# A decoder block in fp32 on one core: another order in the mixer, an earlier split of a weight block, a root with a bias at the end

## The chip, the cores and the metric

The kernel runs on one core of a Trainium2 chip. The metric is the time of one execution on the device in microseconds (us), the median of several runs. Its engines work beside each other, each through its own list of instructions in order: TensorE (PE) multiplies matrices, VectorE (DVE), ScalarE (ACT) and GpSimd (POOL) do the elementwise work, and SyncE (SP) issues the transfers between the main memory and the on-chip buffer SBUF. PE writes its results into eight banks of PSUM. PEld is the part of PE that loads the stationary operand of the next matmul while the present one runs.

## The reference

One token block of 256 rows and 1024 columns goes through a decoder block in fp32:

```
u = rmsnorm(h, norm_mix_pre)
z = u @ w_in                          # p (512) | q (512) | k (512) | v (512) | g (2048)
g = z[..., o_g:] + b_gate;  g_pool, g_attn = g[..., :1024], g[..., 1024:]
y_pool = pool_mixer(p, pool_w, pool_scale) @ w_branch_pool      # causal means over 2, 4, 8, 16 rows
y_attn = moba_attention(q, k, v) @ w_branch_attn                # 256 rows are one block: causal, ALiBi, 8 heads
m = sigmoid(g_pool) * y_pool + sigmoid(g_attn) * y_attn
h = h + rmsnorm(m @ w_out, norm_mix_post)
u2 = rmsnorm(h, norm_mlp_pre)
a = square(relu(u2 @ w_up))                                     # 4096 columns
h = h + rmsnorm(a @ w_down, norm_mlp_post)                      # the output
```

## The kernel before

Every product is made of three matmuls, since each fp32 operand is kept as a rounded part `hi` and a remainder `lo`: hi by hi, lo by hi, hi by lo (`mm3`, L227 to L229; `mm3_wide` with 512 columns, L236 to L240). Weights come from the main memory in blocks of 1 MB, issued by SP into three raw buffers. Each block is split when its turn comes: ACT writes `hi` (L89), and then `lo = raw - hi` (L93) is written by DVE alone, or for most blocks ahead of the MLP by DVE (11/16 of the columns, 1408 per partition) and POOL (5/16, 640 per partition) side by side (`share_lo`). `split_next` takes the next block in the order of use, and issues the load of another into the raw buffer that comes free.

The order on every engine is the order of the code; nothing reorders it. A tile waits for its producers by semaphores.

The stages, in the order in which PE meets them:

- v, q and k. `features(blocks, f2, ...)` makes 256 output columns (a group of 48 matmuls of 256 moving columns, with the weights stationary and the tokens `u` moving). Its hook `early` runs before the splits that it calls, `evac` after them. `evac_k` (L483) multiplies the keys with the row factor on DVE (L434), writes them as `hi` on ACT (L489) and as `lo` on DVE (L490) into the tile `stacked`.
- scores (L522, L523) of two heads at a time, softmax on DVE and ACT, with the slopes of ALiBi in the tile `prob`, filled by POOL (`fill_slopes`, L441).
- p, two groups; between them and behind them fp32 transposes of the probabilities (`turn_probs`).
- the gates, g0 to g3, each of two blocks and two groups of 48 matmuls, written below as g00, g01, g10 and so on to g31. Between them lie the fp32 matmuls of the attention (`attend`), the transposes of probabilities and of the attention's output (`turn_attended`, L316), and `pool_project`, the four small products y of the pooling groups.
- the branch products: `bp` from the pooled y (`yh`, `yl`) and `ba` from the attention (`oT`), four groups of 24 matmuls each, then the output projection, and the MLP with its 8 chunks of 512 columns up and down. In the down product each token tile has two PSUM banks of 512 columns; the last piece of a chunk runs as twelve matmuls of 256 columns (`mm3_quarters`).
- `finish(t)` for each of two token tiles: the squares are summed on ACT, DVE multiplies the gain in, the root follows, and three passes (L876) of 384, 384 and 256 columns scale the rows and add the residual; each is sent out by SP (L877). The second half of the gain is divided between DVE (256 columns) and ACT with POOL (256 columns, L872, L873).

`placed(pool, blocks, tag, name, at)` allots a tile and begins its data `at` elements in, so that its address can be chosen against that of other operands.

Of the kernel before, what the change touches and what calls it, by code (L numbers as in the profile page):

```python
# [16 lines left out]
P = 128  # L17
D = 1024
# [15 lines left out]
def hybrid_block(ctx: ExitStack, tc: tile.TileContext, x, norm_mix_pre, w_in, b_gate, pool_w, pool_scale,  # L34
# [229 lines left out]
    def placed(pool, blocks, tag, name, at, room=128):  # L264


        t = pool.tile([P, blocks * S + room], F32R, tag=tag, name=name)
        return t[:, at:at + blocks * S].rearrange("p (k s) -> p k s", k=blocks)
# [4 lines left out]
    def halves():  # L273
        return [(n, slice(n * 512, (n + 1) * 512)) for n in range(2)]
# [151 lines left out]
    def turn_factors():  # L426
        rps = bank("rr_ps")
        for t in range(NT):
            nc.tensor.transpose(rps[:, t * P:(t + 1) * P], spread[:, t * P:(t + 1) * P], ident)
        nc.vector.tensor_copy(rrow, rps[:, 0:S])  # L430
# [8 lines left out]
    def fill_slopes(heads, eng):  # L439
        for h in heads:  # L440
            eng.tensor_scalar(prob[:, h, :], dist, 2.0 ** (-8.0 * (h + 1) / H), None, op0=ALU.mult)  # L441
# [6 lines left out]
    def features(blocks, f2, evac, name, ahead=2, early=None):  # L448
        ps = bank(f"{name}_ps{f2}")
        for j in range(2):  # L450
            for k in range(KD):
                feature(ps, j, blocks, 2 * f2 + j, k)
        if early:
            early(2 * f2, ps)
        if f2 == 0:
            split_next(ahead)
        if evac:
            evac(2 * f2, ps)
        return ps
# [41 lines left out]
    for f2 in range(2):  # L501
        for k in range(KD):
            feature(qps[f2], 1, bq, 2 * f2 + 1, k)
        evac_q(2 * f2, qps[f2])
    turn_factors()
    fill_slopes(range(4, H), nc.gpsimd)
    features(bk, 0, None, "k", early=evac_k)
    k_ps1 = features(bk, 1, None, "k")


# [37 lines left out]
    def attend(po, hp):  # L548
        for h in range(2 * hp, 2 * hp + 2):
            c = slice(h * DH, (h + 1) * DH)  # L550
            nc.tensor.matmul(po[0][:, c], pTs[h][:, 0:P], v_sb[:, 0, c], start=True, stop=True, skip_group_check=True)
            nc.tensor.matmul(po[1][:, c], pTs[h][:, P:2 * P], v_sb[:, 0, c], start=True, stop=False,
                             skip_group_check=True)
            nc.tensor.matmul(po[1][:, c], pTs[h][:, 2 * P:3 * P], v_sb[:, 1, c], start=False, stop=True,
                             skip_group_check=True)
# [11 lines left out]
    def turn_attended():  # L567
        for t in range(NT):
            c = slice(t * P, (t + 1) * P)
            ps = turn(o_sb[:, t, :], 0, f"ot_ps{t}")  # L570
            parts(oT[0][:, :, c], oT[1][:, :, c], ps.rearrange("p (f s) -> p f s", f=4))
# [40 lines left out]

    def pool_project(g2):
        if not yp:
            yp.extend(placed(mixer, NG, t, t[2:], a) for t, a in (("q_yh", 0), ("k_yl", 16)))
        ps = bank(f"y_ps{g2}")
        for j in range(2):
            g = 2 * g2 + j
            mm3(ps[:, j * S:(j + 1) * S], (pws[0][:, g, :], pws[1][:, g, :]), (ys[0][:, g, :], ys[1][:, g, :]),
                True, True)  # L620
        for j in range(2):
            g = 2 * g2 + j
            v, sc = ps[:, j * S:(j + 1) * S], others[P_SCALE + g]
            nc.scalar.activation(yp[0][:, g, :], v, AF.Copy, scale=sc)
            nc.vector.scalar_tensor_tensor(yp[1][:, g, :], v, sc, yp[0][:, g, :].bitcast(F32),
                                           op0=ALU.mult, op1=ALU.subtract)
# [14 lines left out]
    def gates(i, f2):  # L641
        def evac(f, ps):
            c = 4 * i + f
            for j in range(2):
                nc.scalar.activation(sg[:, c + j, :], sg[:, c + j, :], AF.Sigmoid, bias=others[B_GATE + c + j])

        def early(f, ps):
            by_token(sg[:, 4 * i + f:4 * i + f + 2, :], ps)
            if (i, f2) == (3, 1):
                begin_split()()  # L650
        features(bg[i], f2, evac, f"g{i}", early=early)
# [15 lines left out]
    pool(0)  # L667
    pool(1)
    gates(0, 0)
    attend(po, 0)  # L670
    attend(po, 1)
    gates(0, 1)
    pool(2)
    pool(3)
    turn_probs(2)
    turn_probs(3)
    gates(1, 0)
    attend(po, 2)
    attend(po, 3)
    attended(po)  # L680
    ys_pws = mixer.tile([P, 2, NG, S + P], F32R, tag="prob", name="ys_pws")
    ys = [ys_pws[:, i, :, 0:S] for i in range(2)]
    pws = [ys_pws[:, i, :, S:S + P] for i in range(2)]
    gates(1, 1)
    turn_attended()
    split_pool()
    gates(2, 0)
    pool_project(0)
    gates(2, 1)
    pool_project(1)  # L690

    def broadcast(src, name):
        t = const.tile([P, D], F32, name=name)
# [160 lines left out]
    def finish(t):  # L854

        o = o_out[:, t, :]
        ss = small.tile([P, 3], F32, name="ss")
        rr = small.tile([P, 1], F32, name="rr")

        def gain(a, b):  # L860
            nc.vector.scalar_tensor_tensor(o[:, a:b], pd[t][a // 512][:, a % 512:a % 512 + b - a], r2[t],
                                           g_mlp_post[:, a:b], op0=ALU.mult, op1=ALU.mult)

        nc.gpsimd.memset(ss[:, 2:3], 0.0)
        sumsq_act(pd[t][0], ss[:, 0:1], r2[t])
        gain(0, 512)
        sumsq_act(pd[t][1], ss[:, 1:2], r2[t])
        chain = rstd(ss, rr)
        next(chain)
        next(chain)  # L870
        gain(512, 768)
        nc.scalar.activation(o[:, 768:D], pd[t][1][:, 256:512], AF.Copy, scale=r2[t])  # L872
        nc.gpsimd.tensor_tensor(o[:, 768:D], o[:, 768:D], g_mlp_post[:, 768:D], ALU.mult)  # L873
        run(chain)
        for a, b in ((0, 384), (384, 768), (768, D)):
            nc.vector.scalar_tensor_tensor(o[:, a:b], o[:, a:b], rr, h_sb[:, t, a:b], op0=ALU.mult, op1=ALU.add)  # L876
            nc.sync.dma_start(out[0, t * P:(t + 1) * P, a:b], o[:, a:b])  # L877

    prev, nxt = a0, a1
    for j in range(NCH):  # L880
        last = j == NCH - 1
        for t, k in [(t, k) for t in range(NT) for k in range(4)]:
            if last and t == NT - 1:
                continue
            if not last and (t, k) == (NT - 1, 3):

                mm3_quarters(pd[t], tokens(prev, k, t), wide(bd[j], k))
            else:
                mm3_wide(pd[t], tokens(prev, k, t), wide(bd[j], k), j == 0 and k == 0, last and k == 3)
        split_next(2)  # L890
        if last:
            break
        if j + 2 < NCH:
            a = up_parts(j + 2)
            up_half(j + 2, 0, a)
            up_half(j + 2, 1, a)
        else:
            a = None
        prev, nxt = nxt, a
    finish(0)  # L900
    for n, c in halves():
        for k in range(4):
            h, l = wide(bd[-1], k)
            mm3(pd[1][n], tokens(prev, k, 1), (h[:, c], l[:, c]), False, k == 3)
    finish(1)


# [27 lines left out]
```

## Time and profile before

| | |
|---|---|
| runs, us | 343.43, 343.54, 344.56; median 343.54 |
| the profiled execution | 343.66, of which the span of the trace is 341.89 |
| granted TensorE clock, mean over the span | 0.996 |
| PE busy | 332.6 us, 97% of the span, 2355 matmuls |
| DVE, ACT, POOL busy | 220.7 (65%), 182.8 (53%), 77.3 (23%) |
| moved by DMA | 63.04 MB, mean 184 GB/s |

Times in the rows are in us from the start of the span. A matmul's duration overlaps the next one's, so the rate of PE is read from one start to the next, or from the length of a stretch that holds a whole group. A stretch's count of matmuls takes in those that reach into it, two or three more than were started there.

### The profile page before, as it was taken

What the parts mean: (1) busy time and instruction counts of PE and PEld (TensorE: products, weight loads), DVE (VectorE), ACT (ScalarE), POOL (GpSimd) and SP (SyncE); (2) the same over time, 40 slices, a digit from 0 to 9 for tenths busy, and PEclk for the clock granted to TensorE, in tenths of its full rate; (3) what the DMA queues carried; (4) which work ended last, traced back from release to release, by engine and by line L of the source; (5) the groups of instructions that cost most, each with busy time, mean ns of one, the idle gap of its engine ahead of it and who ended that gap; (6) DMA issues with size and microseconds to landing.
All of it is one profiled execution on the core that took longest, in us unless ns stands there. A gap on an engine that the chain in (4) does not pass through costs nothing.

```text
span 341.9 us, 5763 instructions
## 1 busy us (share of the span) xinstructions
PE 332.6 (97%) x2355; PEld 308.6 (90%) x2355; DVE 220.7 (65%) x288; ACT 182.8 (53%) x257; POOL 77.3 (23%) x70
## 2 busy tenths in 40 slices
PE   8999999999999999999999999999999999999990
PEld 6799999999999999888898998989989899899880
DVE  3799697996476699466686746637366373653545
ACT  3985658765655755076668426354263551644231
POOL 3699965154303000046700000000000000000000
PEclk9999999999999999999999999999999999999998
DMA  7996961654545946806355763907629177180003
GB/s 215 372 314 221 205 227 35 233 153 158 183 166 204 326 168 217 276 1 246 125 156 214 277 215 133 331 29 261 231 83 339 71 247 246 40 330 3 0 0 123
DMA packets 27506, 63.04 MB, mean 184 GB/s; under 512 B 1332, under 2 KB 3160, under 8 KB 27480
## 3 DMA queue, kind: packets, MB, share of 16 engines
q1 hardware_dynamic: 26904, 62.15, 53.0%
q0 software_dynamic: 576, 0.52, 1.2%
q8 instruction: 18, 0.29, 0.3%
q14 instruction: 8, 0.07, 0.1%
HBM read 61.10 MB, written 1.05 MB: 182 GB/s over the span
## 4 chain that ended last, share of the span: by engine, by line
PE 84%; DVE 5%; DMA 4%; ACT 2%; SPq 1%; POOL 1%; issue 1%; DVEq 0%; ACTq 0%; POOLq 0%
PE up_ps L227 9%; PE up_ps L228 9%; PE up_ps L229 9%; PE d_ps L237 7%; PE d_ps L236 7%; PE d_ps L240 7%; PE g_ps L227 4%; PE g_ps L228 4%; PE g_ps L229 4%; DMA v_r<-in_w_in_dram 2%; PE wo_ps L240 2%; PE wo_ps L236 2%; PE wo_ps L237 2%; DMA k_r<-in_w_in_dram 2%; DVE k_l L93 1%; PE bp_ps L228 1%
## 5 line engine op out<-in xcount | busy, mean ns | idle before, releaser
L227 PE MATMUL up_ps<-u2h,up_h 128*128 128x256 f32 x224 | 62.1, 277 | 0.0
L228 PE MATMUL up_ps<-u2l,up_h 128*128 128x256 f32 x224 | 61.9, 276 | 0.0
L229 PE MATMUL up_ps<-u2h,up_l 128*128 128x256 f32 x224 | 61.9, 276 | 0.0
L93 DVE TENSOR_TENSOR dn_l<-dn_r,dn_h 128x2048 fp32r<-128x2048 f32 x16 | 36.5, 2292 | 16.7 <-ACT dn_h L89 16.6
L228 PEld LDWEIGHTS up_ps<-u2l,up_h 128*128 128x128 f32 x224 | 42.1, 188 | 0.0
L227 PEld LDWEIGHTS up_ps<-u2h,up_h 128*128 128x128 f32 x224 | 42.1, 188 | 0.0
L229 PEld LDWEIGHTS up_ps<-u2h,up_l 128*128 128x128 f32 x224 | 42.1, 188 | 0.0
L89 ACT ACTIVATE dn_h<-dn_r 128x2048 fp32r<-128x2048 f32 x16 | 30.5, 1918 | 21.5 <-issue 12.8
L236 PE MATMUL d_ps<-dn_h,ah 128*128 128x512 f32 x106 | 41.3, 390 | 0.0
L237 PE MATMUL d_ps<-dn_l,ah 128*128 128x512 f32 x106 | 41.3, 390 | 0.0
L873 POOL TENSOR_TENSOR o_out<-o_out,g_mlp_post 128x256 f32<-128x256 f32 x2 | 1.5, 728 | 163.7 <-DVE rr L305 159.5
L227 PE MATMUL g_ps<-uh,g_h 128*128 128x256 f32 x128 | 36.1, 282 | 0.0
L228 PE MATMUL g_ps<-ul,g_h 128*128 128x256 f32 x128 | 35.7, 279 | 0.0
L229 PE MATMUL g_ps<-uh,g_l 128*128 128x256 f32 x128 | 35.7, 279 | 0.0
L93 DVE TENSOR_TENSOR up_l<-up_r,up_h 128x2048 fp32r<-128x2048 f32 (+1 forms) x14 | 30.2, 2194 | 8.2 <-ACT up_h L89 8.2
L240 PE MATMUL d_ps<-dn_h,al 128*128 128x512 f32 x106 | 32.6, 389 | 0.0
L89 ACT ACTIVATE up_h<-up_r 128x2048 fp32r<-128x2048 f32 x16 | 29.9, 1907 | 1.6 <-PE wo_ps L240 1.6
L786 ACT ACTIVATE relu<-up_ps 128x512 f32<-128x512 f32 x16 | 9.6, 597 | 39.4 <-PE up_ps L229 39.4
L788 DVE TENSOR_TENSOR a<-up_ps,relu 128x512 f32<-128x512 f32 x16 | 11.1, 691 | 28.8 <-ACT relu L786 28.7
L93 POOL TENSOR_TENSOR up_l<-up_r,up_h 128x640 fp32r<-128x640 f32 (+1 forms) x4 | 15.6, 3909 | 46.7 <-ACT up_h L89 46.7
L227 PEld LDWEIGHTS g_ps<-uh,g_h 128*128 128x128 f32 x128 | 24.3, 190 | 0.0
L228 PEld LDWEIGHTS g_ps<-ul,g_h 128*128 128x128 f32 x128 | 24.1, 188 | 0.0
(231 smaller groups left out, 864.3 us busy)
## 6 DMA issues: line engine op xcount, KB each, us to landing
up_r<-in_w_up_dram SPq DMA_DIRECT2D x16, 1024.0 KB, 5.6
dn_r<-in_w_down_dram SPq DMA_DIRECT2D x16, 1024.0 KB, 5.0
g_r<-in_w_in_dram SPq DMA_DIRECT2D x8, 1024.0 KB, 5.5
o_r<-in_w_out_dram SPq DMA_DIRECT2D x4, 1024.0 KB, 4.8
v_r<-in_w_in_dram SPq DMA_DIRECT2D x8, 256.0 KB, 5.8
q_r<-in_w_in_dram SPq DMA_DIRECT2D x4, 512.0 KB, 6.1
k_r<-in_w_in_dram SPq DMA_DIRECT2D x2, 1024.0 KB, 5.9
p_r<-in_w_in_dram SPq DMA_DIRECT2D x2, 1024.0 KB
```

What stands on the lines that cost most here:

```text
L89: nc.scalar.activation(self.hi[:, s, :], self.raw[:, s, :], AF.Copy)
L93: eng.tensor_tensor(self.lo[:, s, c], self.raw[:, s, c], self.hi[:, s, c].bitcast(F32), ALU.subtract)
L227: nc.tensor.matmul(ps, wh, rh, start=start, stop=False, skip_group_check=True)
L228: nc.tensor.matmul(ps, *second, start=False, stop=False, skip_group_check=True)
L229: nc.tensor.matmul(ps, *third, start=False, stop=stop, skip_group_check=True)
L236: nc.tensor.matmul(ps, xh, wh[:, c], start=start, stop=False, skip_group_check=True)
L237: nc.tensor.matmul(ps, xh, wl[:, c], start=False, stop=False, skip_group_check=True)
L240: nc.tensor.matmul(ps, xl, wh[:, c], start=False, stop=stop, skip_group_check=True)
L786: nc.scalar.activation(r, ps, AF.Relu)
L788: nc.vector.tensor_tensor(a, ps, r, ALU.mult)
L873: nc.gpsimd.tensor_tensor(o[:, 768:D], o[:, 768:D], g_mlp_post[:, 768:D], ALU.mult)
```

## The change

There are five edits.

1. The first block of p is split (ACT, then DVE and POOL) ahead of the read-out of the keys, by a hook that calls `split_next` before `evac_k`; one block is then left to split behind it, and the slopes of heads 4 to 7 move on POOL behind both.
2. In the mixer the group g01 moves ahead of the attention of heads 0 to 3, and g11 ahead of that of heads 4 to 7; both `pool_project` calls come behind g20, and the transposes of the attention's output last, behind them.
3. `yh` and `yl` begin 32 and 112 elements into their tiles in place of 0 and 16. The tile of the pooling operands is laid out flat, with 256 elements of room, and the stationary ones begin 16 elements behind the moving ones.
4. In the down product the piece of chunk 6 that ran as twelve matmuls of 256 columns runs as six of 512.
5. The last token tile has its own end, `finish_last`: the mean's first half is put into a bias (`rest`) while the second half is still multiplied, the root takes the sum of squares of the second half straight from ACT, the gain of the second half is one DVE instruction of 512 columns, and two passes of 512 columns with two transfers of 256 KB close the program.

```diff
+    def split_and_evac_k(f, ps):
+        split_next()
+        evac_k(f, ps)
+
+    features(bk, 0, None, "k", ahead=1, early=split_and_evac_k)
     fill_slopes(range(4, H), nc.gpsimd)
-    features(bk, 0, None, "k", early=evac_k)
     k_ps1 = features(bk, 1, None, "k")
...
-            yp.extend(placed(mixer, NG, t, t[2:], a) for t, a in (("q_yh", 0), ("k_yl", 16)))
+            yp.extend(placed(mixer, NG, t, t[2:], a) for t, a in (("q_yh", 32), ("k_yl", 112)))
...
     gates(0, 0)
+    gates(0, 1)
     attend(po, 0)
     attend(po, 1)
-    gates(0, 1)
     pool(2)
     pool(3)
     turn_probs(2)
     turn_probs(3)
     gates(1, 0)
+    ys_pws = mixer.tile([P, 2 * NG * (S + P) + 256], F32R, tag="prob", name="ys_pws")
+    ys = [ys_pws[:, i * NG * S:(i + 1) * NG * S].rearrange("p (g s) -> p g s", g=NG) for i in range(2)]
+    pws = [ys_pws[:, 2 * NG * S + 16 + i * NG * P:2 * NG * S + 16 + (i + 1) * NG * P].rearrange(
+        "p (g c) -> p g c", g=NG) for i in range(2)]
+    gates(1, 1)
     attend(po, 2)
     attend(po, 3)
     attended(po)
-    ys_pws = mixer.tile([P, 2, NG, S + P], F32R, tag="prob", name="ys_pws")
-    ys = [ys_pws[:, i, :, 0:S] for i in range(2)]
-    pws = [ys_pws[:, i, :, S:S + P] for i in range(2)]
-    gates(1, 1)
-    turn_attended()
     split_pool()
     gates(2, 0)
     pool_project(0)
+    pool_project(1)
+    turn_attended()
     gates(2, 1)
-    pool_project(1)
...
+    def finish_last(t):
+
+        o = o_out[:, t, :]
+        ss = small.tile([P, 3], F32, name="ss")
+        rest, v = (work.tile([P, 1], F32, name=n, bufs=1) for n in ("rest", "rest_v"))
+        for n, c in halves():
+            sumsq_act(pd[t][n], ss[:, n:n + 1], r2[t])
+            nc.vector.scalar_tensor_tensor(o[:, c], pd[t][n], r2[t], g_mlp_post[:, c], op0=ALU.mult, op1=ALU.mult)
+            if n == 0:
+                nc.vector.tensor_scalar(v, ss[:, 0:1], -0.5 / D, -0.5 * EPS, op0=ALU.mult, op1=ALU.add)
+                nc.vector.tensor_scalar(rest, v, -2.0, None, op0=ALU.mult)
+        sq = small.tile([P, 1], F32, name="sq")
+        nc.scalar.activation(sq, ss[:, 1:2], AF.Sqrt, bias=rest, scale=1.0 / D)
+        nc.vector.scalar_tensor_tensor(v, ss[:, 1:2], -0.5 / D, v, op0=ALU.mult, op1=ALU.add)
+        r, a, rr = (small.tile([P, 1], F32, name=n) for n in ("r", "nwt", "rr"))
+        nc.vector.reciprocal(r, sq)
+        nc.vector.scalar_tensor_tensor(a, r, r, v, op0=ALU.mult, op1=ALU.mult)
+        nc.vector.scalar_tensor_tensor(rr, a, 1.5, r, op0=ALU.add, op1=ALU.mult)
+        for n, c in halves():
+            nc.vector.scalar_tensor_tensor(o[:, c], o[:, c], rr, h_sb[:, t, c], op0=ALU.mult, op1=ALU.add)
+            nc.sync.dma_start(out[0, t * P:(t + 1) * P, c], o[:, c])
+
...
-            if not last and (t, k) == (NT - 1, 3):
+            if j + 2 < NCH and (t, k) == (NT - 1, 3):
...
-    finish(1)
+    finish_last(1)
```

Three places show how the rows of an engine move. On DVE, at the read-out of the first keys (`k`, then `stacked`), with `p_l` the remainder of p's two blocks, this stands before:

```order
L430 COPY rrow<-rr_ps 128x256
L434 TENSOR_TENSOR k_558<-k_ps_509,rrow 128x512
L490 TENSOR_TENSOR stacked<-k_558,stacked 64x2x256 x2
L93 TENSOR_TENSOR p_l<-p_r,p_h 128x4x352 x2
L527 SCALAR_TENSOR_TENSOR prob<-s_ps_644,rr_154,prob 128x256
```

and this after the change:

```order
L430 COPY rrow<-rr_ps 128x256
L93 TENSOR_TENSOR p_l<-p_r,p_h 128x4x352
L434 TENSOR_TENSOR k_561<-k_ps_505,rrow 128x512
L490 TENSOR_TENSOR stacked<-k_561,stacked 64x2x256 x2
L93 TENSOR_TENSOR p_l<-p_r,p_h 128x4x352
L532 SCALAR_TENSOR_TENSOR prob<-s_ps_644,rr_154,prob 128x256
```

The first of two `p_l` now stands ahead of the three rows that the keys need, the second stays behind them.

On PE, around the transposes of the attention's output (`ot_ps`), which stand between g11 and g20 before:

```order
L229 MATMUL g_ps_1126<-uh,g_4_l 128x256
L316 MATMUL ot_ps_1178<-ident,o_sb 128x128 x4
L316 MATMUL ot_ps_1185<-ident,o_sb 128x128 x4
L227 MATMUL g_ps_1202<-uh,g_0_h 128x256
L228 MATMUL g_ps_1202<-ul,g_0_h 128x256
L229 MATMUL g_ps_1202<-uh,g_0_l 128x256
```

and behind the products of the pooling (`y_ps`) and ahead of g21 after the change:

```order
L227 MATMUL y_ps_1265<-ys_pws 128x256
L228 MATMUL y_ps_1265<-ys_pws 128x256
L229 MATMUL y_ps_1265<-ys_pws 128x256
L316 MATMUL ot_ps_1276<-ident,o_sb 128x128 x4
L316 MATMUL ot_ps_1283<-ident,o_sb 128x128 x4
L227 MATMUL g_ps_1290<-uh,g_0_h 128x256
L228 MATMUL g_ps_1290<-ul,g_0_h 128x256
L229 MATMUL g_ps_1290<-uh,g_0_l 128x256
```

The transposes change places with y: the group that follows them is g21 where it was g20.

On DVE, the end of the program (`d_ps` is the down product of the last token tile, `ss` its sums of squares), before:

```order
L861 SCALAR_TENSOR_TENSOR o_out<-d_ps_2195,r_1_1732,g_mlp_post 128x512
L294 TENSOR_SCALAR m<-ss 128x1
L299 TENSOR_SCALAR v<-m 128x1
L861 SCALAR_TENSOR_TENSOR o_out<-d_ps_2196,r_1_1732,g_mlp_post 128x256
L302 RECIPROCAL r<-sq 128x1
L304 SCALAR_TENSOR_TENSOR nwt<-r,v 128x1
L305 SCALAR_TENSOR_TENSOR rr<-nwt,r 128x1
L876 SCALAR_TENSOR_TENSOR o_out<-o_out,rr,h_sb 128x384 x2
L876 SCALAR_TENSOR_TENSOR o_out<-o_out,rr,h_sb 128x256
```

and after the change:

```order
L892 SCALAR_TENSOR_TENSOR o_out<-d_ps_2195,r_1_1732,g_mlp_post 128x512
L894 TENSOR_SCALAR rest_v<-ss 128x1
L895 TENSOR_SCALAR rest<-rest_v 128x1
L892 SCALAR_TENSOR_TENSOR o_out<-d_ps_2196,r_1_1732,g_mlp_post 128x512
L898 SCALAR_TENSOR_TENSOR rest_v<-ss,rest_v 128x1
L900 RECIPROCAL r<-sq 128x1
L901 SCALAR_TENSOR_TENSOR nwt<-r,rest_v 128x1
L902 SCALAR_TENSOR_TENSOR rr<-nwt,r 128x1
L904 SCALAR_TENSOR_TENSOR o_out<-o_out,rr,h_sb 128x512 x2
```

The two small rows on the first half now precede the second gain, which has 512 columns; the closing passes are two of 512.

## Rows read from the trace of the kernel before

**Rows 1.** Timeline of PE at scores and p: start us, us, engine, line, operands.

```profile
41.87 0.35 PE L522 MATMUL s_ps<-stacked 128*128 128x256 f32 x1
...
45.33 0.28 PE L228 MATMUL p_ps<-ul,p_h 128*128 128x256 f32 x1
45.73 0.39 PE L229 MATMUL p_ps<-uh,p_l 128*128 128x256 f32 x1
45.95 0.28 PE L227 MATMUL p_ps<-uh,p_h 128*128 128x256 f32 x1
```

**Rows 2.** Instructions on p's blocks: ns min/median/max, first and last start us.

```profile
L89 ACT ACTIVATE p_h<-p_r x2: 1902/1912/1922, 39.0 to 40.9; 128x2048 fp32r<-128x2048 f32 x2
L93 DVE TENSOR_TENSOR p_l<-p_r,p_h x2: 1789/2337/2885, 41.0 to 42.8; 128x1408 fp32r<-128x1408 f32 x2
L93 POOL TENSOR_TENSOR p_l<-p_r,p_h x2: 2262/2601/2940, 41.9 to 44.2; 128x640 fp32r<-128x640 f32 x2
```

**Rows 3.** Timelines of ACT, DVE and POOL around the keys and at a gate's split.

```profile
35.10 0.60 ACT L478 ACTIVATE stacked<-q_ps 64x512 fp32r<-64x512 f32 x1 [0.86 <-DVE ql L480]
...
36.98 0.69 DVE L434 TENSOR_TENSOR k<-k_ps,rrow 128x512 f32<-128x512 f32 x1
38.37 1.41 DVE L490 TENSOR_TENSOR stacked<-k,stacked 64x512 fp32r<-64x512 f32 x2 [0.70 <-ACT stacked L489]
...
54.91 1.63 DVE L93 TENSOR_TENSOR g_l<-g_r,g_h 128x1408 fp32r<-128x1408 f32 x1 [0.47 <-ACT g_h L89]
...
54.96 2.99 POOL L93 TENSOR_TENSOR g_l<-g_r,g_h 128x640 fp32r<-128x640 f32 x1 [6.28 <-ACT g_h L89]
```

**Rows 4.** PE by stretches: start:end, length, busy (matmuls), clock, DMA share, GB/s.

```profile
45.95:49.84 3.89, 3.89 (x34) 1.00 0.95 317
58.73:64.18 5.45, 5.45 (x50) 1.00 0.91 286
66.78:72.52 5.74, 5.74 (x51) 1.00 0.03 4
82.08:87.61 5.53, 5.53 (x50) 1.00 0.77 237
88.40:93.94 5.54, 5.54 (x51) 1.00 0.23 88
94.66:100.31 5.65, 5.65 (x50) 1.00 0.33 95
101.03:112.34 11.31, 11.31 (x99) 1.00 0.57 213
112.34:115.17 2.83, 2.83 (x27) 1.00 1.06 374
115.17:117.89 2.72, 2.72 (x26) 1.00 0.99 389
191.92:202.81 10.89, 10.89 (x98) 1.00 0.94 339
320.32:321.68 1.36, 1.36 (x7) 1.00 0.00 0
321.68:323.12 1.44, 1.44 (x14) 1.00 0.00 0
```

**Rows 5.** Timeline of the end, ACT, DVE and SP's queue.

```profile
334.87 0.19 ACT L279 ACTIVATION_READ_ACCUMULATOR scr_a<-d_ps,r 128x1 f32 x1
...
336.38 0.16 DVE L305 SCALAR_TENSOR_TENSOR rr<-nwt,r 128x1 f32<-128x1 f32 x1
336.57 2.10 DVE L876 SCALAR_TENSOR_TENSOR o_out<-o_out,rr,h_sb 128x384 f32<-128x384 f32 x3
...
337.77 1.36 SPq L877 DMA_DIRECT2D out_dram<-o_out  x3
```

**Rows 6.** Line 762, the same operation with 512 columns: ns min/median/max.

```profile
L762 DVE SCALAR_TENSOR_TENSOR h_sb<-h_sb,rr,x_sb x4: 747/750/754, 148.6 to 160.6; 128x512 f32<-128x512 f32 x4
```

**Rows 7.** Transfers in the last stretch, 338.66 to 340.22 us.

```profile
DMA packets 424, 0.51 MB, mean 328 GB/s; under 512 B 48, under 2 KB 424, under 8 KB 424
```

## The prediction

> **What bounds the kernel now.** I read the busy shares first: PE works in 97% of the span, so time can only come from three things: gaps between matmuls, the pace of one matmul after another, and what lies ahead of the first and behind the last one. The timeline of PE by starts shows the gaps; stretches that hold one whole group show the pace; the timeline of the last microseconds shows the end.
>
> There is one gap that the change touches. In the first group of p the matmul that reads p's second remainder starts 0.40 behind its forerunner and the next 0.22 behind it [rows 1]. It waits for `p_l`, whose second DVE row began at 42.8 and took 2.885, so to 45.7 [rows 2]. That row is long because POOL's first part of `p_l` (41.9 to 44.2) was in work: DVE then needed 1.5 more. Two rows of the same size thus don't run beside each other, the one in work holds the other.
>
> The pace has two levels at the same clock of 1.00. The 96 matmuls of an up product take 10.89, so 0.1134 each, those of g3 11.31, so 0.1178; g00 took 5.45 and g01 5.74, bp 2.83 and ba 2.72, with equal counts [rows 4]. The DMA share doesn't sort them: g01 was slow at 0.03, g00 fast at 0.91. What does sort them is what stands ahead and where operands lie. g01 follows the fp32 matmuls of the attention, and g3 a y and g21 (5.65); g20 follows the transposes of the attention's output and runs at 5.54, 0.1 over 48 by 0.1134, which is 5.44, at the change-over. A group keeps the pace with which it came in. bp and ba differ only in the moving operand: from the sizes of the tiles allotted, the weights begin 224 bytes past a multiple of 512, `u` and `oT` 160, `yh` and `yl` 32 and 288.
>
> The rule against this is in the Trainium skill, TensorE: Matmul & The Clock Gate, "Step-by-step: what each phase is for": the engine has two independent read ports, and loading the next weights takes nothing from the running matmul. By it no address and no order would change the pace; bp's 2.83 against ba's 2.72 speaks against it here, though it doesn't say what causes the difference. What follows if it holds after all is rival A.
>
> **The change part by part.** *The p split.* ACT is free at 35.70 [rows 3]; I take p's first block to have landed by then, since both were there at 39.0 to 40.9, when ACT split them without a pause [rows 2]; were it late, the keys would be late by as much. `p_h` takes 1.91 [rows 2], so to 37.64; `p_l` 1.63 on DVE, as on the first gate [rows 3], to 39.30. Then the keys: 0.69 for `k`, to 40.0. Before, the two `lo` rows ended 1.41 and 2.11 behind `k` (38.37 plus 1.41, less 37.67) [rows 3], so now at 41.4 and 42.1. The scores' first matmul needs the first of them at 41.87 [rows 1], the second head's some 0.5 later: margins 0.45 and about 0.3. So what is moved into the keys' path (2.4 us) is hidden by the second k group, and costs one for one from there. The second `p_h` follows the keys' two `hi` rows (some 0.7 each): to about 43.3, `p_l` to 45.0, due at 45.45 or so: margin 0.5. POOL then has its part of `p_l`, and the slopes of heads 4 to 7 behind both; they are needed only at the third pair of scores, ten microseconds on. The stall goes: 0.62 less two paces of 0.1134, that is -0.39. Behind the stall p ran 33 matmuls in 3.89 [rows 4]; if it stays fast as it came in, 33 by 0.1134 is 3.74: -0.15. Together -0.54.
>
> *The mixer.* g01 follows g00 directly: 5.74 becomes 5.45, -0.29. g11 follows g10, which follows transposes of probabilities and comes in slow: 5.53 becomes 5.65, +0.12. g20 now follows the attention's matmuls. Behind these one group was slow (g01, 5.74) and one fast (g11, 5.53), so I take the middle: +0.09. g21 follows the transposes, as g20 did: 5.65 becomes 5.54, -0.11. g3 keeps that pace: 11.31 becomes 10.89, -0.42. `yh` and `yl` now begin at 160 bytes like `oT`, so bp should run as ba: four times 0.11, -0.44 (there are four such pairs, one stands in the rows). The sum is -1.05. The pooling operands are also placed anew, 24 matmuls in all; I count nothing there (0.1 at most). The bounds: no pace changes, 0, or by +0.2 for g11 and g20 alone; or all go fast, g11 and g20 too: -1.5. I take the value in the middle, since the nearest rows (ba, g20) each show the very case. The waits here: y of groups 2 and 3 now comes 5.65 earlier, and POOL must have written its remainders by then; POOL's work in the mixer is light, and g20 lies between the split and the first y. I count nothing; cover gone, PE would wait for the rest of POOL's four rows.
>
> *The down product.* Six matmuls of 512 take 1.36 and twelve of 256 1.44 [rows 4]: -0.08.
>
> *The end.* ACT's sum of squares is read at 335.06. Before, `rr` was done at 336.54 [rows 5], over a mean, a root and a half gain in turn. Now the root starts without the mean, while DVE's gain of 512 takes 0.75 (as line 762 [rows 6]), 335.09 to 335.84; four small rows of about 0.16 follow: 336.5. So `rr` comes no earlier, and the gain has lost POOL and ACT as helpers at no cost. The passes: three took 2.10 with POOL's multiplication beside the first; the first transfer was issued at 337.77 [rows 5]. Two of 0.75 [rows 6] end at 337.3 and 338.05, so the first issue comes at about 337.3. The first packet came 0.89 behind the issue, 338.66, and 0.51 MB took 1.56 [rows 7]; half of that, 0.78, covers the second pass's lag of 0.75. The end moves with the first issue, -0.45; from 0 (a larger transfer that starts later) to -0.65 (both passes overlap better). I take -0.45.
>
> The sum is -0.54 -1.05 -0.08 -0.45, so -2.12, against the profiled execution's 343.66: 341.5. That execution is 0.12 over the median of the runs shown, which is inside their scatter.
>
> **The rivals.** *A: order and placement don't set the pace.* What counts is then only the stall (-0.39), the down piece and the end: -0.92, so 342.7. For it: the g groups differ in several things at once, and the traces show an order only as it was. Against it: bp and ba, four times alike.
>
> *B: slower, POOL gets to `p_l` first.* Both engines wait for the same `p_h`. If POOL starts first, DVE waits through its 1.41 (44.2 less 42.79 [rows 2]): the keys come 1.41 later than worked out above, 42.8 against a due time of 41.87, and PE waits 0.96 and 0.16 more; the second `p_l`, held in the same way, ends at 47.7 against 46.6: 1.13. Then p costs +2.25 -0.39, +1.86 in place of -0.54: 343.9, above the 343.54 of before. It decides from 0.45 us of lateness on. Against it: at the gate's split DVE began at 54.91, POOL at 54.96 [rows 3], and both are idle here alike. The Trainium skill, SBUF — State Buffer, "SBUF: two separate sides", has the same mechanism: whichever of DVE and GpSimd starts first holds their shared ports for a whole instruction; the 2.885 agrees.
>
> *C: the end gains nothing*, the larger transfers starting later by what is won: 341.95.
>
> *D: all g groups go fast.* If g11 and g20 run at 5.45 and 5.54, -0.29 more, and p's second group and g10, which follow transposes of probabilities as before, gain 0.29 each, as g01: 340.6.
>
> **How the numbers follow.** The forecast, with C inside its range of 340.9 to 342.1, has 0.60; D 0.15; A 0.15; B 0.04; nothing measurable for reasons that I don't see 0.06. What a measurement of this kernel can tell from no change is 0.3%, 1.03 us: faster is below 342.5, slower above 344.6. Faster is then the forecast, D, and a third of A (0.05), where the end gives the 0.2 more that its bound allows: 0.80; same is the rest of A and the last case: 0.16; slower 0.04, from B, and that only where the mixer gives nothing too (343.9 plus 1.05). The range of 340.5 to 342.8 takes in D and A.
>
> **What would show it.** In the trace after, p's first group has no gap over 0.2 and stays at 0.1134; the first `p_l` on DVE takes 1.63 and begins ahead of POOL's; scores start without a wait; g01, g21, g3 and bp come at 5.45, 5.54, 10.89 and 2.72; the first transfer is issued 0.45 earlier against the last matmul's end. Wrong would be: bp still at 2.83 (the placement), g3 at 11.31 (the order), a PE wait for `stacked` or `ys_pws` (a cover gone), or the first packet no earlier against the last matmul.

## The result and the profile after

The changed kernel takes 340.35 us (median of 4 runs, 339.75 to 340.71) beside 343.99 in the same job: a ratio of 0.9897, 95% interval 0.9880 to 0.9913. That is faster, and by more than forecast: 341.5 was the forecast and 340.5 the lower end. The profiled execution took 340.71 with a span of 338.9, so 2.95 less than the profiled one of before; the sum had -2.12. Of the distance between the sum's 341.54 and the median, 1.19, terms of the sum make 0.83, and 0.36 lie between the profiled execution and the median. One execution of e9 (1187.97 us) is left out of its median and ratio below.

Stretches of PE in the trace after, with the columns of [rows 4]: k, p's two groups, g0, g1, g20, g21 with g3, the first bp and ba, and the last six matmuls of chunk 6 in the down product.

```profile
30.71:42.31 11.60, 11.60 (x100) 1.00 0.97 236
44.22:49.68 5.46, 5.46 (x51) 1.00 0.58 188
50.25:55.80 5.55, 5.55 (x52) 1.00 0.14 52
58.31:69.19 10.88, 10.88 (x99) 1.00 0.59 193
73.05:84.03 10.98, 10.98 (x100) 1.00 0.58 193
86.62:92.36 5.74, 5.74 (x50) 1.00 0.42 159
94.57:110.99 16.42, 16.42 (x148) 1.00 0.65 216
110.99:113.71 2.72, 2.72 (x27) 1.00 1.05 364
113.71:116.43 2.72, 2.72 (x27) 1.00 1.03 360
319.87:321.23 1.36, 1.36 (x7) 1.00 0.00 0
```

The same view of the kernel before has k, p's two groups and g10 (not among the rows shown) as follows.

```profile
30.62:41.87 11.25, 11.25 (x100) 1.00 0.95 234
43.84:49.84 6.00, 5.88 (x50) 1.00 0.72 228
50.41:56.15 5.74, 5.74 (x52) 1.00 0.24 93
73.74:79.48 5.74, 5.74 (x51) 1.00 0.91 324
```

Together with [rows 4] the whole difference can be laid out, before to after, with the term of the sum beside it:

| stretch | before, us | after, us | difference | forecast |
|---|---|---|---|---|
| k | 11.25 | 11.60 | +0.35 | 0 |
| p, first group | 6.00 | 5.46 | -0.54 | -0.54 |
| p, second group | 5.74 | 5.55 | -0.19 | 0 |
| g0 (g00 + g01) | 5.45 + 5.74 | 10.88 | -0.31 | -0.29 |
| g1 (g10 + g11) | 5.74 + 5.53 | 10.98 | -0.29 | +0.12 |
| g20 | 5.54 | 5.74 | +0.20 | +0.09 |
| g21 and g3 | 5.65 + 11.31 | 16.42 | -0.54 | -0.53 |
| four bp, four ba | 22.2 | 21.76 | -0.46 | -0.44 |
| output projection to the last matmul's start | 199.24 | 199.14 | -0.10 | -0.08 |
| from the last matmul's start to the end | 8.09 | 7.05 | -1.05 | -0.45 |

The rest, +0.10 at the start, -0.13 in the scores and a few hundredths, makes -2.95. DVE now writes its part of p's remainder without interruption, twice, and begins ahead of POOL by 0.05 (37.76 and 37.81 the first time); the second time:

```profile
43.27 1.63 DVE L93 TENSOR_TENSOR p_l<-p_r,p_h 128x1408 fp32r<-128x1408 f32 x1 [1.19 <-ACT p_h L89]
43.32 3.02 POOL L93 TENSOR_TENSOR p_l<-p_r,p_h 128x640 fp32r<-128x640 f32 x1 [2.51 <-ACT p_h L89]
```

DVE's row takes 1.63 in place of 2.885 and is over at 44.90 in place of 45.67, so PE waits for p no more. k shows what an interruption can do. Its PE rows around its one wait, before and after:

```profile
32.20 0.28 PE L228 MATMUL k_ps<-ul,k_h 128*128 128x256 f32 x1
32.45 0.38 PE L229 MATMUL k_ps<-uh,k_l 128*128 128x256 f32 x1
```

```profile
32.29 0.28 PE L228 MATMUL k_ps<-ul,k_h 128*128 128x256 f32 x1
32.54 0.39 PE L229 MATMUL k_ps<-uh,k_l 128*128 128x256 f32 x1
```

The step of 0.25, where 0.1133 is the pace, is the same in both; but behind it k goes on at 0.1178 after, and went on at 0.1133 before.

The end after (DVE and SP's queue, as in [rows 5]), then the last transfers and what lies behind the last packet in both kernels (the third number from the right is the clock, then DMA share, GB/s):

```profile
334.37 0.16 DVE L902 SCALAR_TENSOR_TENSOR rr<-nwt,r 128x1 f32<-128x1 f32 x1
334.56 1.42 DVE L904 SCALAR_TENSOR_TENSOR o_out<-o_out,rr,h_sb 128x512 f32<-128x512 f32 x2
335.34 1.00 SPq L905 DMA_DIRECT2D out_dram<-o_out  x2
```

```profile
336.17:337.69 1.52, 0.00 (x0) 0.00 (x0) 0.00 (x0) 0.00 (x0) 0.00 (x0) 0.50 0.93 344
337.69:338.94 1.25, 0.00 (x0) 0.00 (x0) 0.00 (x0) 0.00 (x0) 0.00 (x0) 0.50 0.00 0
```

```profile
340.22:341.89 1.67, 0.00 (x0) 0.00 (x0) 0.00 (x0) 0.00 (x0) 0.00 (x0) 0.50 0.00 0
```

From the last matmul's start, `rr` is done at 2.64 (before 2.74), the first issue comes at 3.45 (3.98), the last packet ends at 5.80 (6.42): -0.62 up to there. The other 0.42 lies behind the last packet, where no engine computes: 1.25 in place of 1.67.

### The profile page after: what moved, and what is told of

Read it like the earlier page. It is cut to its first block, busy times and chain, and to the rows that moved or that the text cites. A ratio compares the mean times of both kernels' runs of the same rounds, so it can differ in the third digit from the quotient of the medians.

```text
span 338.9 us, 5743 instructions
## 1 busy us (share of the span) xinstructions
PE 330.7 (98%) x2349; PEld 306.8 (91%) x2349; DVE 219.6 (65%) x288; ACT 181.9 (54%) x256; POOL 79.0 (23%) x68
## 3 DMA queue, kind: packets, MB, share of 16 engines
HBM read 61.10 MB, written 1.05 MB: 183 GB/s over the span
## 4 chain that ended last, share of the span: by engine, by line
PE 96%; DMA 1%; DVE 1%; SPq 0%; DVEq 0%; ACT 0%; issue 0%; ACTq 0%
PE up_ps L227 9%; PE up_ps L229 9%; PE up_ps L228 9%; PE d_ps L237 7%; PE d_ps L236 7%; PE d_ps L240 7%; PE g_ps L227 4%; PE g_ps L228 4%; PE g_ps L229 4%; PE wo_ps L240 2%; PE wo_ps L236 2%; PE wo_ps L237 2%; DMA x_sb<-in_x_dram 1%; PE k_ps L229 1%; PE q_ps L227 1%; PE k_ps L228 1%
## 5 line engine op out<-in xcount | busy, mean ns | idle before, releaser
L236 PE MATMUL d_ps<-dn_h,ah 128*128 128x512 f32 x108 | 42.1, 389 | 0.0
L237 PE MATMUL d_ps<-dn_l,ah 128*128 128x512 f32 x108 | 42.1, 389 | 0.0
L879 POOL TENSOR_TENSOR o_out<-o_out,g_mlp_post 128x256 f32<-128x256 f32 x1 | 0.7, 736 | 159.4 <-ACT o_out L878 159.4
L240 PEld LDWEIGHTS d_ps<-dn_h,al 128*128 128x128 f32 x108 | 20.3, 188 | 4.2
```

The source lines that it names most:

```text
L236: nc.tensor.matmul(ps, xh, wh[:, c], start=start, stop=False, skip_group_check=True)
L237: nc.tensor.matmul(ps, xh, wl[:, c], start=False, stop=False, skip_group_check=True)
L240: nc.tensor.matmul(ps, xl, wh[:, c], start=False, stop=stop, skip_group_check=True)
```

## The experiments

The times scatter by 1 to 3 us within a job, so a ratio's interval is 0.5 to 0.8 us to either side; what a single part does is read from the traces, and the medians say whether the sum agrees.

**The parts alone.** e1: `finish(1)` becomes `finish_last(1)`.

```diff
-    finish(1)
+    finish_last(1)
```

> The kernel before with finish_last in place of finish(1) for the last token tile, nothing else. From the last matmul's start to the end of the trace it was 8.09 us before and 7.05 after the whole change. If the end alone gives that, the time falls by 1.05 and the last stretch is 7.05; by the prediction's sum it would fall by 0.45 (7.64). The PE stream ahead of it is that of before, instruction for instruction. If the order of the stages or the operands' places set the pace of a group, its groups show the paces of before once more: p's second group 5.74, g01 5.74, g10 5.74, g11 5.53, g20 5.54, g21 5.65, g3 11.31. If the pace is a matter of chance at each interruption, some of these differ in this trace.

342.66 us against 343.53, ratio 0.9975 (0.9957 to 0.9994). From the last matmul's start to the end: 7.04, with 1.25 behind the last packet. The end alone gives the 1.05. From p's second group on the PE stream repeats the paces of before; three of its groups (g01, g10, g3):

```profile
68.56:74.30 5.74, 5.74 (x50) 1.00 0.02 4
75.53:81.27 5.74, 5.74 (x52) 1.00 0.91 327
102.82:114.13 11.31, 11.31 (x99) 1.00 0.63 212
```

e2: the first of the change's hunks alone.

```diff
+    features(bk, 0, None, "k", ahead=1, early=split_and_evac_k)
     fill_slopes(range(4, H), nc.gpsimd)
-    features(bk, 0, None, "k", early=evac_k)
```

> The kernel before with the first block of p split ahead of the read-out of the keys, nothing else. The gap in p's first group goes (0.39) and the group takes 5.46 in place of 6.00: -0.54. In the trace of the whole change k took 0.34 more than before, in its second part, at the slow pace from its one wait on. If the early split is what slows k, k is slow here too and the gain is 0.2; if that was chance, k has either pace here. The mixer's groups have the same neighbours as before: by the order theory their paces are those of before.

342.87, ratio 0.9981 (0.9962 to 1.0000). k had no wait and was fast (10.99). In e5, e8 and e9 below, which have the early split and the wait, k goes on fast behind it (11.25 to 11.30), so the early split is not what slows k. p's two groups and then g10 and g11 in its trace:

```profile
43.91:49.35 5.44, 5.44 (x50) 1.00 0.60 182
49.92:55.47 5.55, 5.55 (x51) 1.00 0.07 28
72.98:78.53 5.55, 5.55 (x51) 1.00 0.82 300
81.13:86.87 5.74, 5.74 (x51) 1.00 0.78 255
```

The groups g10 and g11 have the neighbours of before and yet the opposite paces: 5.55 and 5.74 where before had 5.74 and 5.53, and e1 5.74 and 5.54. So the stage directly ahead doesn't set the pace; a fast p is felt as far as g11.

e3 and e4: the order without the places, and the places without the order.

```diff
 # e3
     gates(0, 0)
+    gates(0, 1)
     attend(po, 0)
     attend(po, 1)
-    gates(0, 1)
...
     pool_project(0)
+    pool_project(1)
+    turn_attended()
     gates(2, 1)
-    pool_project(1)
 # e4
-            yp.extend(placed(mixer, NG, t, t[2:], a) for t, a in (("q_yh", 0), ("k_yl", 16)))
+            yp.extend(placed(mixer, NG, t, t[2:], a) for t, a in (("q_yh", 32), ("k_yl", 112)))
...
+    ys_pws = mixer.tile([P, 2 * NG * (S + P) + 256], F32R, tag="prob", name="ys_pws")
```

> The kernel before with the mixer's new order (g01 and g11 ahead of the attention, both products of the pooling ahead of the transposes), with the places of yh, yl and the pooling operands as before. By the prediction's terms -0.61 (g01 -0.29, g11 +0.12, g20 +0.09, g21 -0.11, g3 -0.42); by the trace of the whole change -0.94 (g0 -0.31, g1 -0.29, g20 +0.20, g21 and g3 -0.54). bp stays at 2.83 in all four. If only chance sets the pace behind an interruption, g1, g20 and g3 may come out either way, but there are fewer interruptions, so fewer slow groups on average.

> The kernel before with yh and yl at 32 and 112 and with the pooling operands laid out flat, the order as before. bp falls from 2.83 to 2.72, four times: -0.44, if the place alone sets it. If bp is slow because of the slow g3 ahead of it, it stays at 2.83 here and the time doesn't move.

e3: 342.64, ratio 0.9973 (0.9957 to 0.9988); e4: 342.27, ratio 0.9963 (0.9947 to 0.9979). By the medians e1 to e4 give -0.87, -0.66, -0.89 and -1.26, together -3.68, in which what g21 and g3 gain (about 0.6, see below) is counted twice; the whole change gave -3.27 in the second job (c_after). The shorter piece of chunk 6 had no run of its own. g21 with g3 and the first bp in e3:

```profile
95.06:111.48 16.42, 16.42 (x148) 1.00 0.66 216
111.48:114.31 2.83, 2.83 (x27) 1.00 1.05 359
```

g21, g3 and the first bp in e4:

```profile
94.08:99.52 5.44, 5.44 (x50) 1.00 0.22 82
100.20:111.08 10.88, 10.88 (x98) 1.00 0.77 264
111.08:113.80 2.72, 2.72 (x26) 1.00 1.05 385
```

bp's pace is its operands' place. But the places do more than was expected of e4: with the pooling operands laid out anew, y itself is fast (0.68 in place of 0.72), and g21 and g3 behind it are fast in the old order as well. That y hands its pace on fits this, but it is no rule for all groups: each ba is fast (2.72) behind a slow bp. The new order does the same for g21 and g3 with y still at 0.72, by the transposes between. The change pays for these 0.6 us twice and gets them once.

Both traces also show something about waits. In e4, whose program is that of before up to there, p waits longer than before (0.58 from start to start in place of 0.40), and yet goes on fast; its first group, with the wait, and its second:

```profile
43.53:49.55 6.02, 5.72 (x50) 1.00 0.69 218
50.13:55.67 5.54, 5.54 (x51) 1.00 0.28 108
```

e13 below does the same (6.03, then 5.55). So the wait and the slow pace behind it are two things: the slow pace came of it before and in e1, not in e4 and e13. In e3 the first scores start 0.74 late:

```profile
42.71 0.36 PE L522 MATMUL s_ps<-stacked 128*128 128x256 f32 x1 [0.58 <-DMA stacked<-stacked]
```

They wait for the copies of the queries that POOL sends into `stacked` (L479). By the trace's semaphore records the first copy had landed at 42.57 there, and at 41.72 in the kernel before, 0.15 ahead of its first score.

**What sets the pace.** c_after is the changed kernel unedited; e5 and e6 move one operand each.

```diff
 # e5
-            yp.extend(placed(mixer, NG, t, t[2:], a) for t, a in (("q_yh", 32), ("k_yl", 112)))
+            yp.extend(placed(mixer, NG, t, t[2:], a) for t, a in (("q_yh", 0), ("k_yl", 16)))
 # e6
-    u = tuple(placed(act, KD, f"uT_{i}", f"u{i}", 112) for i in "hl")
+    u = tuple(placed(act, KD, f"uT_{i}", f"u{i}", 128) for i in "hl")
```

> The changed kernel once more, nothing edited: a second trace of it. If the pace of each group is set by what the program holds (order, operands), all groups come out as in the first trace: k's second part slow from its wait on, p fast, g0 and g1 fast, g20 slow at 5.74, y at 1.42, g21 and g3 fast. If it is chance at every interruption, several differ. If only a wait for another engine leaves it open, k alone may differ, and the groups from g0 on are the same.

> The changed kernel with yh and yl back at 0 and 16. If the place of the moving operand sets bp's pace, bp is 2.83 in all four groups, each ba behind it comes back to 2.72, and the time rises by 0.44 over the changed kernel. If the pace is only carried in from the group ahead (g3 fast), bp stays at 2.72 and the time does not move.

> The changed kernel with u placed 128 elements into its tile in place of 112, so that it begins 224 bytes past a multiple of 512, as the weights do, in place of 160. If the distance between moving operand and weights sets whether the fast pace exists, all of q, k, p and the gates run at about 117.8 or slower: 672 matmuls less the 130 that are slow already, by 4.45 ns: +2.4 us, and bp and ba stay fast. If only order and chance set the pace, the time does not move.

c_after: 340.39, ratio 0.9900 (0.9877 to 0.9922); e5: 340.75, 0.9908 (0.9885 to 0.9930); e6: 344.21, 1.0017 (1.0002 to 1.0032). In c_after every group from p on has the pace of the first trace to 0.01, and k is slow again. In e5, whose program is the same up to bp, k was fast behind its wait (11.30), the g groups as in c_after; in e7, e8 and e10 they are the same once more. So here the program sets the pace of the groups that follow one another without a wait; a wait on another engine leaves it open. bp and then ba in e5:

```profile
110.95:113.78 2.83, 2.83 (x27) 1.00 1.04 392
113.78:116.50 2.72, 2.72 (x26) 1.00 1.04 367
```

g0, then g21 with g3, then the first bp in e6:

```profile
59.72:71.23 11.51, 11.51 (x99) 1.00 0.47 169
97.30:114.65 17.35, 17.35 (x148) 1.00 0.63 216
114.65:117.39 2.74, 2.74 (x27) 1.00 1.01 389
```

With u moved by 64 bytes no group on u is fast; 11.51 over 96 is 0.1199. bp and ba, whose operands were not moved, are fast. For the places tried here the place decides whether the fast pace exists, and e6 costs more than was expected (from q's first matmul to the output projection 116.6 us, in the trace after 113.2; 2.4 more were expected), since the slow pace there is slower still.

e13 puts transposes into the old order: a `pad` of `features` that transposes `ident` into the group's bank.

```diff
+        for _ in range(pad):
+            nc.tensor.transpose(ps[:, 0:P], ident, ident)
...
+        features(bg[i], f2, evac, f"g{i}", early=early, pad=1 if (i, f2) in ((2, 1), (3, 0)) else 0)
```

> The kernel before with one transpose of 128 by 128 more ahead of g21 and one ahead of g30, each behind a product y of the pooling; order and places as before. If a transpose gives the fast pace back wherever it stands, g21 with it takes 5.57 in place of 5.66 and g3 with it 11.01 in place of 11.31: -0.39. If it was the new order as a whole, or the place of the pooling operands, that freed g21 and g3, they stay at 5.66 and 11.31 and the time rises by 0.05 to 0.2. bp stays at 2.83 in both.

343.61, ratio 1.0003 (0.9983 to 1.0022). g21 with its transpose, then g3 with its own:

```profile
94.65:100.42 5.77, 5.77 (x52) 1.00 0.35 110
101.14:112.14 11.00, 11.00 (x99) 1.00 0.60 206
```

g21 stays slow and is 0.11 longer by the transpose, g3 is fast. The same insertion failed behind the first y and worked behind the second. A single transpose is no sure cure; which insertion gives the fast pace back stays a matter of trying.

**The waits ahead of the scores.** e11 takes `bp` out of the list of shared blocks; e7 shares k's first block; e10 moves k's first remainder into a pause of DVE.

```diff
 # e11
-    shared = [b for g in bb + bg[0:3] + [bq, bp, bo, bu[0], bu[1]] for b in g]
+    shared = [b for g in bb + bg[0:3] + [bq, bo, bu[0], bu[1]] for b in g]
 # e7
-        bk[0].split_lo(nc.vector)
+        bk[0].share_lo(0)
 # e10
-        for _ in range(3):
+        for i in range(3):
+            if i == 2:
+                bk[0].split_lo(nc.vector)
             for c in chains:
                 next(c)
...
-        bk[0].split_lo(nc.vector)
```

> The changed kernel with the remainders of both p blocks written by DVE alone (2.58 us in place of 1.63, POOL writes nothing). It takes the keys' read-out 0.95 later, beyond the margin of 0.45 that was worked out, or 0.2 more where k is slow: PE should wait 0.5 or so ahead of the first scores on the keys' remainder, and no longer, since POOL is out of the way and p's remainder is then whole at 42.2. If the margin was mis-sized by more than 0.5, no wait shows.

> The changed kernel with the remainder of the first k block shared between DVE and POOL, as other blocks' are, in place of DVE alone. DVE has its second k remainder done about 0.8 us earlier, at about 31.6 in place of 32.4, so the wait of PE in k (0.25) goes, and with no interruption k stays fast, as q is: k takes 10.98 in place of 11.60, -0.6. The slopes on POOL and the copies of q behind them start 1.4 us later; if the scores wait for those copies, the gain is lost. If k's slow pace doesn't come from the wait, only -0.25.

> The changed kernel with DVE's first remainder of k (2.58 us) moved ahead of the row factors' last small rows, into the 1.2 us in which DVE waits for the root on ACT. DVE's second k remainder then ends about 0.5 earlier, at 31.8 in place of 32.3; PE's wait of 0.25 in k goes. If that wait is what leaves k's pace open, k now keeps the fast pace that it has ahead of it: k takes 10.98 in place of 11.60, -0.6 against the changed kernel. If k stays slow without the wait, something else sets it, and the gain is 0.25. Against it: v's read-out on ACT needs the row factors, which come some 2 us later; if q's read-out is held by that, a wait moves to the keys.

e11 (one run, 341.23) shows the margin's size; its waits of PEld from 30 to 60 us:

```profile
PEld p_ps L229 <- DVE p_l L93: 0.2, 1, 0.2
PEld s_ps L527 <- DVE stacked L490: 0.2, 1, 0.2
```

DVE alone took 2.29 there, 0.66 more than 1.63, and a wait of 0.2 came of it, at the second pair of scores: the margins that were worked out, 0.45 for the first pair and about 0.3 for the second, were of the right size. p went on slow behind its wait, and so did p's second group (5.74), as before the change.

e7: 340.74, 0.9915 (0.9894 to 0.9935), no gain. POOL's new row holds up a row of DVE that needs 0.22; DVE, then POOL:

```profile
25.50 1.31 DVE L304 SCALAR_TENSOR_TENSOR nwt<-r,v 128x1 f32<-128x1 f32 x1
```

```profile
25.23 1.57 POOL L93 TENSOR_TENSOR k_l<-k_r,k_h 128x640 fp32r<-128x640 f32 x1
```

DVE gets on only when POOL is through at 26.80, 1.1 late, and PE's wait in k grows to 0.5. The first scores are 0.2 late as well: the first copy of the queries lands at 42.11, and they start at 42.24. e10: 340.24, 0.9921 (0.9902 to 0.9940). Its trace has no wait of PE from 30 to 60 us, and k stays fast, 10.99 in place of 11.60:

```profile
30.59:41.58 10.99, 10.99 (x100) 1.00 0.81 197
```

k's second remainder is whole at 30.99 there, 1.5 earlier than in the first trace after the change (32.49). One trace doesn't show that the edit was needed: e2 and e11 have no wait in k and a fast k without it, since the start of DVE's rows scatters (second remainder whole at 31.79 and 32.00). In the four traces without the wait and with u in its place (e2, e10, e11, e12) k is fast; with it, it was slow in the two traces of the unedited changed kernel alone.

**The end.** e8 keeps the new root and gain and divides the closing passes as before.

```diff
-        for n, c in halves():
+        for c in (slice(0, 384), slice(384, 768), slice(768, D)):
```

> The changed kernel with the closing passes and transfers divided as before, 384, 384 and 256 columns, the root with the bias and the whole gain on DVE kept. In the changed kernel the stretch from the last matmul's start to the end is 7.05: first issue at 3.45, last packet at 5.80, and 1.25 behind it; before it was 3.98, 6.42 and 1.67. If the 0.42 behind the last packet come from the place of the last transfer's wait in SP's closing list of waits (one transfer fewer shifts it), three transfers bring them back: 1.67 behind the last packet. If they come from the root, the gain or the missing POOL and ACT rows, it stays at 1.25. The first pass has 384 columns and ends about 0.2 earlier than one of 512, so the first issue comes at about 3.25, and the last packet at 5.6 to 5.8. Sum 7.3 to 7.45 by the first theory, 6.9 to 7.05 by the second.

341.42, 0.9946 (0.9926 to 0.9966). The last packet ends at 5.76 behind the last matmul's start, no later than with two; behind it:

```profile
339.32:341.14 1.82, 0.00 (x0) 0.00 (x0) 0.00 (x0) 0.00 (x0) 0.00 (x0) 0.50 0.00 0
```

The trace's records of SP tell why. SP closes the program with a list of waits, on the semaphores that its transfers signal, 0.06 apart. Its rows with two transfers (the first trace after the change) and with three (e8), by number, ns min/median/max, first and last start:

```profile
L958 SPq EVENT_SEMAPHORE  x10: 17/28/28, 336.4 to 338.9; - x10
```

```profile
L958 SPq EVENT_SEMAPHORE  x10: 17/28/28, 339.8 to 341.1; - x10
```

With two the list is begun 4.5 behind the last matmul's start, with three only at 6.27, when the last transfer has landed. With three transfers the last one signals a semaphore (102) near the head of the list: in e8 that wait is over at 6.27, seven more follow it, and SP is through them at 6.75; before, it is over at 6.92, with five more, up to 7.27. With two transfers the last one signals the semaphore at the end of the list (110): all others are over by 5.54, this one at 6.16, and SP is through at 6.23. So the number of transfers moved that wait's place in the list, 0.42 in e8 and 0.28 against before. The rest, 0.14, is the landing of the last transfer, whose wait is over 0.50 behind its last packet with three and 0.36 with two; why that differs is not shown. Together that makes 0.57 in e8, 0.42 against before.

**Both ways on.** e9 puts one transpose ahead of g20 (as in e13, with `(i, f2) == (2, 0)`), e12 is e9 and e10 together.

> The changed kernel with one fp32 transpose of 128 by 128 more, behind the attention of heads 4 to 7 and ahead of g20, into the bank that g20 then overwrites. It costs about 0.11 on PE. In all traces so far a group that follows the attention's matmuls alone changes its pace: fast becomes slow, slow becomes fast; with transposes between, g1 came out fast behind a fast g0. If the transposes' row is what gives the fast pace back, g20 falls from 5.74 to 5.54, together -0.09. If only their number (12 or 8) does it or the attention's own end counts, g20 stays at 5.74 and the time rises by 0.11. The groups ahead of it are as before it in both cases.

> The changed kernel with both edits that sped PE up in their traces: k's first remainder earlier on DVE, and one transpose of 128 by 128 ahead of g20. If the two add up, PE's stretch from q's first matmul to the output projection's first one is 112.3 in place of 113.1 (k -0.6, or -0.4 where k happened to be fast; g20 and y -0.18), with every group from q on at the fast pace, and the time falls by 0.6 to 0.8 against the changed kernel, by the trace more surely than by the median, since the start of the program scatters by more. If g20's pace depends on when it starts rather than on what stands ahead, it may be slow again.

e9: 340.51, 0.9928 (0.9911 to 0.9945); g20 with the transpose takes 5.57 in place of 5.74 and y behind it 1.36 in place of 1.42. The transpose costs 0.03 from its start to the next one's, 0.06 with what the row ahead of it loses, not 0.11. e12: 339.98, 0.9894 (0.9871 to 0.9917). k, g20 and the whole stretch from q to the output projection in e12, and that stretch in c_after:

```profile
30.80:41.79 10.99, 10.99 (x99) 1.00 0.82 210
86.02:91.59 5.57, 5.57 (x51) 1.00 0.39 149
19.66:131.93 112.27, 112.27 (x993) 1.00 0.62 202
```

```profile
19.41:132.53 113.12, 113.11 (x992) 1.00 0.61 200
```

All groups from q on are fast, and PE is 0.85 shorter, as expected. By its time e12 beats the kernel before; against the changed kernel (340.35 and 340.39) the 0.4 is within the scatter, so that it beats that one too is shown by the trace only.

## Why the prediction was wrong

- *The direction and most terms were right.* p's gap and pace (-0.54), g0 (-0.31), g21 and g3 (-0.54), bp (-0.46) and the down piece came to within 0.02 of their terms. Rivals A, B and C fell: the pace did move, DVE was ahead of POOL, the end did gain. D came nearest, with p's second group and g1 fast as it said, though g20 was not; its terms add up to 340.7, not 340.6.
- *The step that failed first: "The end moves with the first issue, -0.45".* It measured -1.05. Up to the last packet the gain was -0.62, inside the bound of -0.65: the issue came 0.53 earlier, the first packet followed it by 0.83 as before, and the packets took 1.52 in place of 1.61. (The prediction's 0.89 and 1.56 are read from a stretch that begins 0.06 behind the first packet; their sum is right.) The missing 0.42 was a part of the end that the sum held fixed, what SP still waits for behind the last packet. The bounds that were set for this term, 0 and -0.65, took in the passes and transfers alone. e1 shows the size, e8 the cause, but for the 0.14 of the landing.
- *The step that failed next: "A group keeps the pace with which it came in", and each stage ahead given the pace that it once showed.* "g11 ... comes in slow ... +0.12" was wrong, and p's second group was counted at nothing. That group had been slow before because p went slow at its wait: with p fast it is fast in every trace (e2, e3, e4, e13 and those after the change). So removing the wait was worth more than its own group, -0.19 behind it, measured against an execution in which p went slow there; e4 and e13 show that it need not. g1's -0.29 is the new order's: in the old one either g10 or g11 was slow (e1, e2), in the new one both are fast, in e3 and also in e11, where p is slow (10.98).
- *g20, taken in the middle at +0.09, came out at +0.20*, in the same direction; k's +0.35 was in no term. It arose behind the wait in k, which was there before and which the sum leaves out; k happened to go on fast there.
- *Against the range.* The profiled execution, 340.71, would have been inside. It is the slowest of the four runs of that job; k's pace behind the wait differs between kernels that are the same up to there, which fits runs of 339.75 beside it, though no trace of such a run shows it. To land inside would have been luck: k's +0.35 covers a part of what the other terms gained over the sum. With the end at -1.05 and g1 at its measured -0.29 the sum is -3.13 and the forecast 340.5.
- *The scores.* The margins of 0.45 and 0.3 counted the keys alone. The scores need the copies of the queries as well, and these landed only 0.15 ahead of the first score before. They cost nothing in the trace after the change, 0.2 in e7 and 0.74 in e3; the sum has no term for them.
- *What the prediction drew from the rule on two independent ports* (the Trainium skill, TensorE: Matmul & The Clock Gate, "Step-by-step: what each phase is for"), that no address would change the pace, doesn't hold here: e6 changes nothing but the address of `u`, and the stretch up to the output projection takes 3.4 us more. Whether the ports themselves are independent, and why some distances cost, is not shown by any run.

## What to carry to other kernels

Where PE never pauses, look at its start-to-start interval by group: two levels at one granted clock are time to be had, by placing the moving operand against the stationary one, and by removing short waits, since each can leave a slow pace behind it for several us. Lay the end out to the last record, not to the last packet: what the queue's engine still waits for behind it is time too, and one transfer fewer may move it. When two engines are to share a job, check first that they run beside each other.

## What the runs showed that was not expected

- The fp32r matmul of 256 columns ran at 0.1133, 0.1178 or (e6) 0.120 from start to start, at a granted clock of 1.00 throughout.
- A group can change its pace without a wait, and a wait can free it. Before, p and g00 come in behind scores at 0.118, and their first steps are 0.124, 0.118 or 0.119, then 0.113; g01 and g10 stay at 0.117 to 0.119 from the second step on. In e7 k runs at 0.118 ahead of its wait and at 0.113 behind it.
- The attention's fp32 matmuls exchanged the two paces in every trace with u in its place where nothing stood between: fast g00 gave a slow g01 (5.74), slow g10 a fast g11 (5.53), fast g10 a slow g11 (e2), fast g1 a slow g20 (5.74). The transposes of the attention's output were followed by a fast group in every trace with u in its place.
- An fp32 transpose of 128 by 128 just ahead of a group is 0.03 from the group's start, where transposes among themselves are 0.11 apart. In all it cost 0.06 behind the attention's matmuls (e9) and 0.11 behind a y (e13).
- DVE and POOL did not overlap on the remainders: in shared form 1.63 for DVE and then 1.41 more for POOL, 2.28 to 2.58 for DVE alone.
